# A reserve of early products, a decay multiplied on POOL and joint state updates in a hybrid mixer layer

## The chip, the cores and the metric

The kernel runs on one core of one Trainium2 chip. The metric is the device time of one execution in microseconds (us), lower is better. Five engines work side by side, each in the order of its own instructions: TensorE (PE, with its weight loads as PEld), VectorE (DVE), ScalarE (ACT), GpSimd (POOL) and SyncE (SP), which here issues nearly all transfers, one after the other.

## The reference

One layer of a diffusion backbone on 384 tokens (128 of context, 256 latent), width 2048, in fp32:

```python
h = rmsnorm(x, norm_g) * (1 + scale) + shift          # shift, scale, gate = silu(c) @ ada_w + ada_b
z = h @ w_in                                          # 2048 -> some 18,800 columns
# branch A, 32 heads of 64, two directions, per token t:
sa = S @ a_t
S  = S * w_t[None, :] + sa[:, None] * b_t + v_t[:, None] * k_t
y  = S @ r_t                                          # directions summed, group norm, + bonus
y_a = (norm(y) * silu(g_a)) @ w_out_a
# branch B: short convolution
y_b = (b_gate * conv3(c_gate * x_b) * silu(g_b)) @ w_out_b
out = x + gate * ((sigmoid(m_a) * y_a + sigmoid(m_b) * y_b) @ w_o)
```

The latent scans start from cached states; the final states of the context scans are outputs too. The outputs are the two token groups and the two final states.

## The kernel before

Every large product is made from three reduced-precision products (`mm3`, L81 to L83): a matrix is split into a high and a low part (`split`, L88 the high one on ACT, L89 the low one on DVE), and hi x hi, lo x hi and hi x lo are added in PSUM. A *triple* is these three matmuls for one block of 128 x 128 weights and 384 tokens.

**Prologue.** Eight groups g produce the modulated input `h_hi`/`h_lo`, two of its 16 blocks of 128 rows each. For each group four chunks of adaLN weights (`raw_adah`, 2 transfers of 512 KB, five buffers) are multiplied on PE (L289); `make_h` (L349 to L361) turns the rows by four small matmuls, and DVE and ACT modulate the block and split it. Between the chunks `pops(n)` places *early products*: triples of seven column tiles of w_in that need only the blocks which are there already (`pe`, 14 a group, from a queue). What is left of them stands behind the last `make_h`. Then begins a stream of weights.

**Stream.** `ds_.go(n)` places n triples of the big projection (pairs of column tiles of rk, gv, bc, bx, bg, gb, ma, mb, and ob of w_out_b at the end). `urgent` and `fills` hold what comes next; the weights of a pair are transferred one half at a time (`raw`, two buffers).

**Scan.** Sixteen iterations b, each with a pair of heads, use the stream as filler. In chunks of 64 tokens, six a direction: `prep_a` makes keys `bk`, decays `ep` and others, for the next b; `prep_b` makes pA = bk x pr (L687), masks it on DVE (L693) into A, sends triangles to DRAM, inverts them on DVE (L708, L710, 30 steps, tile U), copies the result on POOL (UT, L714) and loads x and A back; `prep_c` transposes bk into `bt` (pb, L754). `scan` begins with a *corner*: pH (L789), copies of x alternating ACT and DVE (L795), H0 = 5 triples, pbn and bon, pX (L789), copies of A (L806), H1 triples. Then two chains walk through the chunks of context (two) and latent tokens (four): po (L827), addition to sav (L828), ls = decayed state (L832, ACT), ytok (L837, L839), pq (L844), copy to sav (L846), pu (L851), new state st (L855 or L857). CH0 triples stand between the steps of the chains while both run, CH1 for the rest of the longer one. `norm` (L896 to L906) and `finish` (L912 to L917) follow, the latter inside the next iteration. An iteration has WINDOW = 80 triples ahead of its scan, FIRST more in the first, LAST in the last; 160 in all in most of them.

At the end the products with w_out_b (ob), w_out_a (oa), the gate rows and w_o follow; `load_yb` and `load_ya` (L500 to L502) bring branch results back from DRAM and split them.

PE's order is the order in which the program is written. That of the other engines is decided by a scheduler, which gives the scan precedence (`high_priority`).

Of the kernel before, what the change touches and what calls it, by code (L numbers as in the profile page):

```python
# [12 lines left out]
ALU = mybir.AluOpType  # L13
AX = mybir.AxisListType

P = 128
# [4 lines left out]
NB = 16  # L21
C = 64
NCH = 6
# [33 lines left out]
def hybrid_step(ctx, tc, cst, x_prompt, x_sample, state_f, state_b, c, c_ctx, ada_w, ada_b, norm_g,  # L57
# [32 lines left out]
        return hi, lo  # L90


    PB0, PB1, H0, H1, CH0, CH1 = 14, 6, 5, 4, 2, 3
    PRO, WINDOW, FIRST, LAST = 32, 80, 12, 16

    def wload(view, k0, cols, nm):

# [267 lines left out]
    def pops(n):  # L365
        for _ in range(n):
            if queue:
                early_mm(*queue.pop(0))

    for g in range(8):  # L370
        m5 = pp.tile([NSEL, 512], F32, tag="m5", name=f"m5_{g}", bufs=2)
        pa = pps.tile([P, 512], F32, tag="ada", name=f"pada_{g}")
        ac = [(256 * g, 256), (D + 256 * g, 256)]
        steps = ada_rows(condw, m5, ac, pa, lambda i: ada_load(pp, f"h{g}", ac, i, 5))
        for j in range(4):
            next(steps)
            if g == 0:
                if j < 3:
                    x_norm(j)
                    x_turn(j)  # L380
                else:
                    make_par()
            if j == 1:
                hl = early_load(g)
            pops(4 if j < 2 else 3)
        make_h(g, m5, pa)
        queue += [(2 * g + e, hl, i) for e in range(2) for i in range(NE)]


# [179 lines left out]
    st = []  # L569
# [87 lines left out]
    def prep_b(b, o):  # L657
# [23 lines left out]
        for d in range(2):  # L681
# [14 lines left out]
            for e in range(2):  # L696
                es = slice(32 * e, 32 * e + 32)
                for h in range(2):
                    hs = slice(C * h + 32 * e, C * h + 32 * e + 32)
                    nc.sync.dma_start(ui[d, e, h::2].rearrange("i s t -> s i t"), A[es, NCH * d:NCH * d + NCH, 0, hs])  # L700

        U = sp.tile([48, 32, 32], F32, tag="U", name=f"U_{b}")
        nc.sync.dma_start(U[:], ui[:].rearrange("d e i s t -> (d e i) s t"))
        ut = sp.tile([48, 256], F32, tag="ut", name=f"ut_{b}")
# [75 lines left out]
    def scan(b, o):  # L780
# [34 lines left out]
        def chain(ch):  # L815
            ls = None
            for i in range((2, 4)[ch]):
                n0 = [((0, 2), (4, 0))[d][ch] + i for d in range(2)]
                f0, step = n0[0], NCH + n0[1] - n0[0]
                fs, ff = slice(f0, f0 + step + 1, step), [f0, f0 + step]  # L820
                lam = [o["ep"][d][:, f % NCH, C:C + 1] for d, f in enumerate(ff)]
                zero = ch == 0 and i == 0
                need_state = ch == 0 or i < 3
                if not zero:
                    po = bank(f"po_{b}_{ch}_{i}")
                    for d, f in enumerate(ff):
                        TE.matmul(po[:, d, :], o["pr"][d][:, f % NCH, :], st[ch][:, d, :], start=True, stop=True)  # L827
                    V.tensor_tensor(sav[0:C, fs, :], po[0:C, 0:2, :], sav[0:C, fs, :], ALU.add)  # L828
                    if need_state:
                        ls = sp.tile([P, 2, P], F32, tag=f"lam{ch}", name=f"ls_{b}_{ch}_{i}")  # L830
                        for d in range(2):
                            S.mul(ls[:, d, :], st[ch][:, d, :], lam[d])  # L832
                    for d, f in enumerate(ff):
                        m = f if d == 0 else 5 - f % NCH
                        dst = ytok[hss[m % 2], m // 2, :]
                        if m in written:
                            V.tensor_tensor(dst, po[C:P, d, :], dst, ALU.add)  # L837
                        else:
                            S.copy(dst, po[C:P, d, :])  # L839
                        written.add(m)  # L840
                    yield 0
                pq = bank(f"pq_{b}_{ch}_{i}")
                for d, f in enumerate(ff):
                    TE.matmul(pq[:, d, :], A[:, f, 0, :], sav[:, f, :], start=True, stop=True)  # L844
                for h in range(2):
                    S.copy(sav[0:C, fs, hss[h]], pq[hss[h], 0:2, hss[h]])  # L846
                yield 0
                if need_state:
                    pu = bank(f"pu_{b}_{ch}_{i}")
                    for d, f in enumerate(ff):  # L850
                        TE.matmul(pu[:, d, :], bt[:, f, :], sav[:, f, :], start=True, stop=True)  # L851
                    for d in range(2):
                        for hs in hss:
                            if zero:
                                V.tensor_scalar(st[ch][hs, d, hs], pu[hs, d, hs], lam[d][hs], None, ALU.mult)  # L855
                            else:
                                V.scalar_tensor_tensor(st[ch][hs, d, hs], pu[hs, d, hs], lam[d][hs],  # L857
                                                       ls[hs, d, hs], ALU.mult, ALU.add)
                    yield 0

        live = [chain(1), chain(0)]
# [71 lines left out]
    for b in range(NB):  # L933
        if b < NB - 1:
            if b > 0:
                ds_.urgent += [(add_rk, b + 1), (add_gv, b)]
        else:
            ds_.urgent += [(add_gv, b)]
        if b == NB - 2:
            ds_.fills += [(add_ob, g) for g in range(8)]  # L940
        pb_gen = prep_b(b, cur)
        ds_.go(next(pb_gen))
        if prev is not None:
# [196 lines left out]
```

## Time and profile before

| | us |
|---|---|
| median of 3 runs | 2289.15 (2288.56 to 2292.72) |
| the profiled execution | 2289.19 |
| its span | 2287.4 |
| PE busy | 2215.7 (97%) |
| DVE busy | 1577.0 (69%) |
| ACT busy | 1017.4 (44%) |
| POOL busy | 104.8 (5%) |

The span is the time from the first to the last instruction; 1.8 us lie around it. The page's slices (a fortieth of the span, 57.2 us, each) show the DMA engines busy at nine tenths or more in the first two, at 335 and 346 GB/s, and at 109 to 134 GB/s in most of the middle. PE shows nine tenths or more in all slices but the first and the last. Busy time of PE counts a matmul from its start to a modelled end: a matmul that is held up halfway counts as busy.

### The profile page before, as it was taken

The page shows a single profiled execution, that of the slowest core. Times are in us where ns is not written, and L with a number is a line of the kernel's source. Part 1 is how long each engine was busy: PE and PEld are TensorE (multiplying, and loading weights), DVE is VectorE, ACT ScalarE, POOL GpSimd, SP SyncE. Part 2 cuts the span into 40 slices and gives each one's busy share as a digit, 9 for nine tenths or more (in the row PEclk, how much of TensorE's full clock was granted, in tenths as well). Part 3 has the DMA queues.
Part 4 walks back from the last instruction along what each step waited for, and adds up shares of the span by engine and source line. Part 5 has one row for each costly group of instructions (what it writes and reads, how often), then busy time and mean ns, then how long its engine had stood idle before and what let it go on. Part 6 is the DMA issues. An engine that isn't in the chain of part 4 may idle for free.

```text
span 2287.4 us, 40741 instructions
## 1 busy us (share of the span) xinstructions
PE 2215.7 (97%) x16084; PEld 2085.5 (91%) x16084; DVE 1577.0 (69%) x3256; ACT 1017.4 (44%) x1836; POOL 104.8 (5%) x99
## 2 busy tenths in 40 slices
PE   6999999999999999999999999999999999999998
PEld 4678899999999999999999999999999999989988
DVE  3248777887777878787878777777778675444444
ACT  4236344444545445444544454545444543333233
POOL 2000000000000000000000000000000000000000
PEclk9999999999999999999999999999999999999999
DMA  9963344434343434343444434444434466786633
GB/s 335 346 190 109 115 110 119 113 113 129 106 119 119 122 108 129 107 125 97 128 111 121 125 115 134 124 126 124 134 112 135 128 217 193 243 299 196 225 129 114
DMA packets 431695, 339.99 MB, mean 149 GB/s; under 512 B 86848, under 2 KB 413072, under 8 KB 430608
## 3 DMA queue, kind: packets, MB, share of 16 engines
q1 hardware_dynamic: 430016, 335.63, 49.1%
q8 instruction: 127, 2.08, 0.4%
q10 hardware_dynamic: 432, 1.57, 0.2%
q14 instruction: 64, 0.52, 0.1%
q0 software_dynamic: 1056, 0.19, 0.1%
HBM read 307.37 MB, written 29.36 MB: 147 GB/s over the span
## 4 chain that ended last, share of the span: by engine, by line
PE 75%; DVE 14%; DMA 4%; ACT 4%; issue 2%; SPq 1%; POOL 0%; POOLq 0%; DVEq 0%; ACTq 0%
PE d_rk L81 3%; PE d_rk L82 3%; PE d_rk L83 3%; PE d_gv L82 3%; PE d_gv L81 3%; PE d_gv L83 3%; DVE st L857 2%; PE d_oa L81 2%; PE pA L687 2%; PE d_oa L83 2%; PE d_oa L82 2%; PE d_bc L81 2%; PE d_ob L81 2%; PE d_ob L83 2%; PE d_ob L82 2%
## 5 line engine op out<-in xcount | busy, mean ns | idle before, releaser
L708 DVE TENSOR_TENSOR ut<-U 48x30 f32<-48x30 f32 (+14 forms) x480 | 154.1, 321 | 18.8 <-DMA U<-ui 7.4
L81 PE MATMUL d_rk<-h_hi,whi_rk 128*128 128x384 f32 x480 | 161.0, 335 | 0.6 <-ACT lst L547 0.6
L81 PE MATMUL d_gv<-h_hi,whi_gv 128*128 128x384 f32 x480 | 161.3, 336 | 0.0
L82 PE MATMUL d_gv<-h_lo,whi_gv 128*128 128x384 f32 x480 | 161.1, 336 | 0.0
L83 PE MATMUL d_gv<-h_hi,wlo_gv 128*128 128x384 f32 x480 | 161.1, 336 | 0.0
L710 DVE TENSOR_TENSOR U<-U,ut 48x30 f32<-48x30 f32 (+14 forms) x480 | 153.8, 320 | 10.1
L82 PE MATMUL d_rk<-h_lo,whi_rk 128*128 128x384 f32 x480 | 160.5, 334 | 0.0
L83 PE MATMUL d_rk<-h_hi,wlo_rk 128*128 128x384 f32 x480 | 160.4, 334 | 0.0
L88 ACT CAST whi_gv<-raw_gv 128x1024 fp32r<-128x1024 f32 (+1 forms) x64 | 64.0, 1000 | 137.0 <-PE d_rk L82 96.4
L89 DVE TENSOR_TENSOR wlo_rk<-raw_rk,whi_rk 128x1024 fp32r<-128x1024 f32 x60 | 73.2, 1223 | 73.9 <-ACT whi_rk L88 73.2
L88 ACT CAST whi_rk<-raw_rk 128x1024 fp32r<-128x1024 f32 x60 | 62.7, 1049 | 91.1 <-PE d_rk L82 28.1
L81 PE MATMUL d_bg<-h_hi,whi_bg 128*128 128x384 f32 x256 | 93.4, 365 | 2.4 <-DVE bc L460 2.4
L81 PE MATMUL d_bc<-h_hi,whi_bc 128*128 128x384 f32 x256 | 93.3, 365 | 0.0
L81 PE MATMUL d_ma<-h_hi,whi_ma 128*128 128x384 f32 x256 | 93.3, 364 | 0.0
L89 DVE TENSOR_TENSOR wlo_oa<-raw_oa,whi_oa 128x1024 fp32r<-128x1024 f32 x32 | 39.2, 1224 | 78.4 <-ACT whi_oa L88 78.4
L81 PE MATMUL d_mb<-h_hi,whi_mb 128*128 128x384 f32 x256 | 93.0, 363 | 0.0
L81 PE MATMUL d_gb<-h_hi,whi_gb 128*128 128x384 f32 x256 | 92.8, 363 | 0.0
L81 PE MATMUL d_bx<-h_hi,whi_bx 128*128 128x384 f32 x256 | 92.1, 360 | 0.0
L81 PEld LDWEIGHTS d_rk<-h_hi,whi_rk 128*128 128x128 f32 x480 | 90.1, 188 | 1.0 <-ACT lst L547 0.9
L81 PEld LDWEIGHTS d_gv<-h_hi,whi_gv 128*128 128x128 f32 x480 | 90.8, 189 | 0.0
L82 PEld LDWEIGHTS d_gv<-h_lo,whi_gv 128*128 128x128 f32 x480 | 90.8, 189 | 0.0
L83 PEld LDWEIGHTS d_gv<-h_hi,wlo_gv 128*128 128x128 f32 x480 | 90.7, 189 | 0.0
(319 smaller groups left out, 6676.6 us busy)
## 6 DMA issues: line engine op xcount, KB each, us to landing
raw_adah<-in_ada_w_dram SPq DMA_DIRECT2D x64, 512.0 KB, 8.7
raw_rk<-in_w_in_dram SPq DMA_DIRECT2D x60, 512.0 KB, 5.4
raw_gv<-in_w_in_dram SPq DMA_DIRECT2D x60, 512.0 KB, 4.5
raw_bc<-in_w_in_dram SPq DMA_DIRECT2D x16, 1024.0 KB, 5.4
raw_bx<-in_w_in_dram SPq DMA_DIRECT2D x16, 1024.0 KB, 5.4
raw_bg<-in_w_in_dram SPq DMA_DIRECT2D x16, 1024.0 KB, 5.4
raw_gb<-in_w_in_dram SPq DMA_DIRECT2D x16, 1024.0 KB, 5.5
raw_ma<-in_w_in_dram SPq DMA_DIRECT2D x16, 1024.0 KB, 5.5
```

What stands on the lines that cost most here:

```text
L81: TE.matmul(out, wh, xh, start=start, stop=False)
L82: TE.matmul(out, wh, xl, start=False, stop=False)
L83: TE.matmul(out, wl, xh, start=False, stop=stop)
L88: S.copy(hi[0:rows], src)
L89: V.tensor_tensor(lo[0:rows], src, hi[0:rows].bitcast(F32), ALU.subtract)
L687: TE.matmul(pas[h, n // 4 * 4][:, n % 4, :], bk[hss[h], n, :], pr[hss[h], n, :], start=True, stop=True)
L708: V.tensor_tensor(tv, U[:, 0:s, s:s + 1].broadcast_to([48, s, w]), U[:, s:s + 1, s + 1:].broadcast_to([48, s, w]), ALU.mult)
L710: V.tensor_tensor(U[:, 0:s, s + 1:], U[:, 0:s, s + 1:], tv, ALU.add)
L857: V.scalar_tensor_tensor(st[ch][hs, d, hs], pu[hs, d, hs], lam[d][hs], ls[hs, d, hs], ALU.mult, ALU.add)
```

## The change

1. *Prologue.* `pops` places 3, 4, 3 and 2 early products behind the four chunks and 2 behind `make_h` (before: 4, 4, 3, 3 and none); in group 1 two behind each. Six products more stay in the queue from there on, and stand behind the last `make_h`.
2. *Decay.* The state update multiplied pu and the old state by the chunk's decay `lam`. Now POOL multiplies the keys `bk` by it once per direction and iteration (128 x 768), behind pA and ahead of the transposes; pu then holds the decay already.
3. *State update.* Four DVE operations on 64 x 64 become two on 64 x 2 x 64: a copy in the first step of the context chain, else an addition of ls.
4. *Numbers.* H1 4 to 2, CH1 3 to 4, FIRST 12 to 24.
5. *Queue.* The last `add_gv` is placed ahead of the eight `add_ob` at b = 14, not as urgent at b = 15.

```diff
@@ -90,8 +90,8 @@
         return hi, lo
 
 
-    PB0, PB1, H0, H1, CH0, CH1 = 14, 6, 5, 4, 2, 3
-    PRO, WINDOW, FIRST, LAST = 32, 80, 12, 16
+    PB0, PB1, H0, H1, CH0, CH1 = 14, 6, 5, 2, 2, 4
+    PRO, WINDOW, FIRST, LAST = 32, 80, 24, 16
 
     def wload(view, k0, cols, nm):
 
@@ -382,8 +382,10 @@
                     make_par()
             if j == 1:
                 hl = early_load(g)
-            pops(4 if j < 2 else 3)
+
+            pops(2 if g == 1 else (3, 4, 3, 2)[j])
         make_h(g, m5, pa)
+        pops(2)
         queue += [(2 * g + e, hl, i) for e in range(2) for i in range(NE)]
 
 
@@ -699,6 +701,9 @@
                     hs = slice(C * h + 32 * e, C * h + 32 * e + 32)
                     nc.sync.dma_start(ui[d, e, h::2].rearrange("i s t -> s i t"), A[es, NCH * d:NCH * d + NCH, 0, hs])
 
+        for d in range(2):
+            G.tensor_tensor(o["bk"][d][:], o["bk"][d][:], o["ep"][d][:, :, C:C + 1].broadcast_to([P, NCH, P]), ALU.mult)
+
         U = sp.tile([48, 32, 32], F32, tag="U", name=f"U_{b}")
         nc.sync.dma_start(U[:], ui[:].rearrange("d e i s t -> (d e i) s t"))
         ut = sp.tile([48, 256], F32, tag="ut", name=f"ut_{b}")
@@ -849,13 +854,11 @@
                     pu = bank(f"pu_{b}_{ch}_{i}")
                     for d, f in enumerate(ff):
                         TE.matmul(pu[:, d, :], bt[:, f, :], sav[:, f, :], start=True, stop=True)
-                    for d in range(2):
-                        for hs in hss:
-                            if zero:
-                                V.tensor_scalar(st[ch][hs, d, hs], pu[hs, d, hs], lam[d][hs], None, ALU.mult)
-                            else:
-                                V.scalar_tensor_tensor(st[ch][hs, d, hs], pu[hs, d, hs], lam[d][hs],
-                                                       ls[hs, d, hs], ALU.mult, ALU.add)
+                    for hs in hss:
+                        if zero:
+                            V.tensor_copy(st[ch][hs, :, hs], pu[hs, 0:2, hs])
+                        else:
+                            V.tensor_tensor(st[ch][hs, :, hs], pu[hs, 0:2, hs], ls[hs, :, hs], ALU.add)
                     yield 0
 
         live = [chain(1), chain(0)]
@@ -934,10 +937,8 @@
         if b < NB - 1:
             if b > 0:
                 ds_.urgent += [(add_rk, b + 1), (add_gv, b)]
-        else:
-            ds_.urgent += [(add_gv, b)]
         if b == NB - 2:
-            ds_.fills += [(add_ob, g) for g in range(8)]
+            ds_.fills += [(add_gv, NB - 1)] + [(add_ob, g) for g in range(8)]
         pb_gen = prep_b(b, cur)
         ds_.go(next(pb_gen))
         if prev is not None:
```

On DVE, the corner of iteration 12 before (kd and kn belong to the next iteration's keys, `x` to L795, `A` to L806):

```order
L649 TENSOR_SCALAR kd_0_16080<-sig_2_16047,par,omka 128x384
L636 RECIPROCAL kn_16070<-kn_16070 128x128
L795 COPY x_12_15583<-pH_16092 32x6x32
L636 RECIPROCAL kn_16070<-kn_16070 128x128
L795 COPY x_12_15583<-pH_16092 32x6x32
L636 RECIPROCAL kn_16070<-kn_16070 128x128
L802 TENSOR_TENSOR bon_16149<-pbn_16146,v_14809 128x384
L637 SCALAR_TENSOR_TENSOR kn_16070<-kk_15975,kn_16070 128x384
L806 COPY A_15419<-pX_16151 32x6x32
L650 TENSOR_TENSOR kd_0_16080<-k_15837,kd_0_16080 128x384
L806 COPY A_15419<-pX_16151 32x6x32
L651 TENSOR_TENSOR sig_2_16047<-kn_16070,sig_2_16047 128x384
```

and after:

```order
L651 TENSOR_SCALAR kd_0_16110<-sig_2_16077,par,omka 128x384
L638 RECIPROCAL kn_16100<-kn_16100 128x128 x3
L800 COPY x_12_15625<-pH_16122 32x6x32
L639 SCALAR_TENSOR_TENSOR kn_16100<-kk_16005,kn_16100 128x384
L800 COPY x_12_15625<-pH_16122 32x6x32
L652 TENSOR_TENSOR kd_0_16110<-k_15867,kd_0_16110 128x384
L653 TENSOR_TENSOR sig_2_16077<-kn_16100,sig_2_16077 128x384
L807 TENSOR_TENSOR bon_16179<-pbn_16176,v_14847 128x384
L646 SCALAR_TENSOR_TENSOR L_1_16114<-cs,sig_1_16053 128x384
L811 COPY A_15459<-pX_16181 32x6x32
L89 TENSOR_TENSOR wlo_mb_0_0_16166<-raw_mb_0_16163,whi_mb_0_0_16165 128x1024
L833 TENSOR_TENSOR sav_15640<-po_1_0_16217,sav_15640 64x2x128
L811 COPY A_15459<-pX_16181 32x6x32
```

The three reciprocals stand together ahead of the first copy of x, one multiplication stands between the two copies of x, and four operations between the second of them and the first copy of A.

On DVE, the early state updates of iteration 12 before (`st_1144` and `st_1146` are the states of the two chains, `sig`, `kd` and `bk` parts of the next keys):

```order
L89 TENSOR_TENSOR wlo_ma_0_1_16140<-raw_ma_0_16133,whi_ma_0_1_16139 128x1024
L651 TENSOR_TENSOR sig_3_16059<-kn_16070,sig_3_16059 128x384
L855 TENSOR_SCALAR st_1144<-pu_0_0_16230,ep_1152 64x64 x2
L855 TENSOR_SCALAR st_1144<-pu_0_0_16230,ep_1154 64x64 x2
L666 TENSOR_TENSOR bk_0_16498<-kd_0_16080,sig_0_16011 128x6x64
L857 SCALAR_TENSOR_TENSOR st_1146<-pu_1_0_16246,ep_1152,ls_1_0_16197 64x64 x2
L857 SCALAR_TENSOR_TENSOR st_1146<-pu_1_0_16246,ep_1154,ls_1_0_16197 64x64 x2
```

and after:

```order
L667 TENSOR_TENSOR bk_1_16539<-sig_3_16089,sig_1_16053 128x6x64
L668 TENSOR_TENSOR bk_1_16539<-kd_1_16118,sig_1_16053 128x6x64
L775 TENSOR_TENSOR kd_0_16110<-kd_0_16110,kd_1_16118 128x384
L859 COPY st_1144<-pu_0_0_16254 64x2x64 x2
L89 TENSOR_TENSOR wlo_mb_0_1_16170<-raw_mb_0_16163,whi_mb_0_1_16169 128x1024
L861 TENSOR_TENSOR st_1146<-pu_1_0_16265,ls_1_0_16221 64x2x64 x2
```

The second update moves behind a split, and the keys' operations ahead of the first.

On PE, the last `make_h` of the prologue before (`pada` is its PSUM tile, `pe` the banks of the early products, `ehi` and `elo` their weights, numbered by group):

```order
L81 MATMUL pe_101<-h_hi_79,ehi_6_830 128x384
L82 MATMUL pe_101<-h_lo_83,ehi_6_830 128x384
L83 MATMUL pe_101<-h_hi_79,elo_6_831 128x384
L349 MATMUL pada_896<-cs,m_7_895 128x2
L350 MATMUL pada_896<-cs,m_7_895 128x2
L349 MATMUL pada_896<-cs,m_7_895 128x2
L350 MATMUL pada_896<-cs,m_7_895 128x2
L81 MATMUL pe_95<-h_hi_79,ehi_7_930 128x384
L82 MATMUL pe_95<-h_lo_83,ehi_7_930 128x384
L83 MATMUL pe_95<-h_hi_79,elo_7_931 128x384
L81 MATMUL pe_96<-h_hi_79,ehi_7_930 128x384
```

and after:

```order
L81 MATMUL pe_95<-h_hi_79,ehi_6_815 128x384
L82 MATMUL pe_95<-h_lo_83,ehi_6_815 128x384
L83 MATMUL pe_95<-h_hi_79,elo_6_816 128x384
L349 MATMUL pada_884<-cs,m_7_883 128x2
L350 MATMUL pada_884<-cs,m_7_883 128x2
L349 MATMUL pada_884<-cs,m_7_883 128x2
L350 MATMUL pada_884<-cs,m_7_883 128x2
L81 MATMUL pe_96<-h_hi_79,ehi_6_815 128x384
L82 MATMUL pe_96<-h_lo_83,ehi_6_815 128x384
L83 MATMUL pe_96<-h_hi_79,elo_6_816 128x384
L81 MATMUL pe_97<-h_hi_79,ehi_6_815 128x384
```

The products behind `make_h` are still of the group before (`ehi_6`), where they were of the new one (`ehi_7`).

## Rows read from the trace of the kernel before

**Rows 1.** Waits of PE: waited for what: us in total, times, longest us.
```profile
PE po L827 <- DVE st L857: 8.9, 14, 1.1
PE pe L81 <- ACT h_hi L360: 7.4, 8, 2.1
...
PE pH L789 <- DMA x<-uo: 5.2, 4, 2.2
PE py L912 <- DVE ytok L906: 3.0, 3, 1.6
...
PE d_ob L81 <- ACT whi_ob L88: 2.3, 1, 2.3
PE d_ob L83 <- DVE wlo_ob L89: 2.1, 2, 1.5
```

**Rows 2.** Groups, 400 to 1800: count, busy us, mean ns, idle before, releaser.
```profile
L857 DVE SCALAR_TENSOR_TENSOR st<-pu,ep,ls 64x64 f32<-64x64 f32 x210 | 59.4, 283 | 14.5 <-PE pu L851 9.5
...
L827 PE MATMUL po<-st,pr 128*128 128x128 f32 x264 | 54.7, 302 | 11.0 <-DVE st L857 8.4
...
L844 PE MATMUL pq<-sav,A 128*128 128x128 f32 x316 | 48.1, 274 | 0.8 <-DVE sav L828 0.8
...
L837 DVE TENSOR_TENSOR ytok<-po,ytok 64x128 f32<-64x128 f32 x54 | 15.9, 294 | 1.2
```

**Rows 3.** Timeline of PE, iteration 12: start, us, instruction, [idle before <- releaser].
```profile
1575.05 1.02 PE L827 MATMUL po<-st,pr 128*128 128x128 f32 x4 [0.46 <-DVE st L857]
```

**Rows 4.** Prologue end: SP issues, transfers from 100 to 140, timeline of PE.
```profile
121.03 4.74 SPq L275 DMA_DIRECT2D raw_adah<-in_ada_w_dram  x4
...
raw_adah<-in_ada_w_dram SPq DMA_DIRECT2D x14, 512.0 KB, 8.5
...
136.74 1.07 PE L289 MATMUL pada<-raw_adah,condw_pro 128*32 128x512 f32 x8
...
150.82 0.33 PE L81 MATMUL pe<-h_hi,ehi 128*128 128x384 f32 x1
...
151.34 0.33 PE L81 MATMUL pe<-h_hi,ehi 128*128 128x384 f32 x1
...
152.64 0.45 PE L81 MATMUL d_rk<-h_hi,whi_rk 128*128 128x384 f32 x1 [0.61 <-ACT lst L547]
```

**Rows 5.** Stretches: us, busy us (x instructions) of five engines, PEclk, DMA share, GB/s.
```profile
369.00:373.00 4.00, 4.00 (x16) 3.97 (x14) 3.88 (x8) 1.36 (x2) 0.00 (x0) 0.57 0.75 254
262.00:266.00 4.00, 1.85 (x55) 1.50 (x54) 1.57 (x2) 0.52 (x3) 0.00 (x0) 1.00 0.79 202
```

**Rows 6.** Corner of iteration 12, timelines of DVE, then PE.
```profile
1551.50 0.94 DVE L636 RECIPROCAL kn<-kn 128x128 f32<-128x128 f32 x1
...
1553.84 0.36 DVE L795 COPY x<-pH 32x192 f32<-32x192 f32 x1
...
1554.25 0.62 PE L789 MATMUL pX<-A,x 32*32 32x32 f32 x48
...
1558.49 0.61 PE L844 MATMUL pq<-sav,A 128*128 128x128 f32 x4
```

**Rows 7.** Corner of iteration 1, timeline of DVE.
```profile
367.28 2.57 DVE L636 RECIPROCAL kn<-kn 128x128 f32<-128x128 f32 x3
...
370.85 0.36 DVE L795 COPY x<-pH 32x192 f32<-32x192 f32 x1
```

**Rows 8.** Timelines: POOL and DVE after an inversion; PE around pA and pb.
```profile
1641.04 2.07 POOL L714 COPY UT<-U 48x1024 f32<-48x1024 f32 x1 [26.84 <-DVE U L710]
...
1641.06 3.15 DVE L89 TENSOR_TENSOR wlo_ma<-raw_ma,whi_ma 128x1024 fp32r<-128x1024 f32 x1
1645.21 1.22 DVE L89 TENSOR_TENSOR wlo_ma<-raw_ma,whi_ma 128x1024 fp32r<-128x1024 f32 x1 [1.01 <-ACT whi_ma L88]
...
1494.59 1.61 PE L687 MATMUL pA<-pr,bk 64*128 64x128 f32 x24
...
1501.07 0.60 PE L754 MATMUL pb<-cs,bk 128*128 128x128 f32 x4
```

## The prediction

> **What bounds the kernel now.** I read the page's shares first: TensorE (PE) is busy 97% of a 2287.4 us span, VectorE (DVE) 69%, so only what PE waits for, or runs slowly through, can be won. Then the waits of PE [rows 1]: none is over 12 us in total, and six of them are near this change (8.9 for the state, 5.2 for x, 3.0 for ytok, 7.4 for h_hi, 2.3 and 2.1 for w_out_b). A matmul that stops between its parts shows no wait, only a longer time, so the groups of the middle come next [rows 2]: po and pq are the same matmul shape, 302 ns against 274. At the pq rate 264 po would take 264 x 48.1/316 = 40.2 us; they take 54.7, so 14.5 us hide inside po, and 11.0 of idle stand ahead of them: 25.5 us in 13.1 iterations, 1.9 each. A late step of iteration 12 shows it [rows 3]: po stands 0.46 us for the DVE's st, and then takes 1.02 us for its four matmuls, where pq takes 0.61 [rows 6], because the second direction's st ends still later.
>
> The profiled run took 2289.19 us, 0.04 from the median of the runs, so the sum is made from 2289.2.
>
> **State update.** Five updates an iteration go from four operations on 64 x 64 (283 ns each, 1.1 us together) to two on 64 x 128. The ytok addition has that shape and those operands, 294 ns [rows 2], so 0.6 us, about half. The decay that they no longer apply goes to POOL. po of the late steps missed its place by at most 0.46 + (1.02 - 0.61) = 0.87 us [rows 3]; 0.5 is saved there and the long direction's fill grows from three triples to four (one triple of matmuls is 0.52 us, from 150.82 to 151.34 in [rows 4]), together 1.0. In the early steps the excess is 0.2 to 0.3, under 0.5. DVE is occupied without a pause from the corner to there, and in the new order the second early update stands behind a 1.22 us split [rows 8]; adding up its operations puts its end at 1566.2 where po wants it at 1566.1, so 0.1 stays in some iterations. I take 24 of the 25.5; the bounds are 12 (only half of each wait goes) and 25.5. The triples in an iteration stay 160, so moving them costs no matmul.
>
> **Decay on POOL.** Two products of 128 x 768 an iteration. No row shows one. Bounds: the DVE's own rate for a two-operand 128 x 1024 (1.22 us [rows 8]) gives 0.92; POOL's copy of 48 x 1024 in 2.07 us gives 1.55; the worst is one that takes 3.1 like the disturbed split of the same rows. I take 1.55. The keys are last read by the second pA, which begins at 1494.59 and ends near 1496.2, and are next read by the transposes from 1501.07 [rows 8]: 4.9 us, and the first product can begin with the first half, 4.8 us sooner. Even 3.1 for the second is covered. If the DVE's masks of pA were held as well, U and with it x would come up to 3 us later; x is waited for in four iterations only [rows 1], so two or three would feel it. Cost taken: 0, bounds 0 to 5.
> What the two engines do to each other is seen where POOL's UT copy and a DVE split start together [rows 8]: 2.07 us on POOL, and 3.15 on the DVE instead of 1.22, so the one ran after the other. The Trainium skill, "GPSIMD Engine Reference", section 1 (Specifications) and section 8 (Key points), says that the two share their SBUF interfaces, and that DVE instructions with two SBUF inputs contend; this trace agrees. The masks read one operand from PSUM: by that rule they would not be held and the sum stays; were they held, it would be 5 us more. [...]
>
> **The corner.** This is what the change costs. Now nothing waits there: in iteration 12 pX starts at 1554.25, just after the DVE's second copy of x has ended (1553.84 + 0.36) [rows 6]. Before, the three reciprocals (0.94 each) alternate with the x copies. In the new order, in iterations 3, 5, 7 and 9 to 14, all three stand first, then copy, multiply, copy. Iteration 1 of before already has this order: three reciprocals from 367.28, last copy ended at 370.85 + 0.36 = 371.21, 3.93 us later [rows 7]. From 1551.50 that is 1555.43, and pX, whose fourth small matmul needs that copy, stops for 1555.43 + 0.05 - 1554.25 = 1.23 us (in iteration 1 it cost nothing only because pX came at half clock). The fill after pX falls by two triples, but pq still comes at 1558.49 + 1.23 - 1.05 = 1558.67 [rows 6], and the A copy that it needs ends at 1558.2 (1555.46, then kd, sig, bon at 0.47 each, a scan of 0.97, the copy 0.36): no second stop. In iterations 4 and 8 a split of 1.22 stands ahead of that A copy: 1.05 more, 2.3. In 2 and 6 one more product of 0.5 stands between the x copies and pq waits 0.55: 2.35. Iteration 0: 1.2. Sum 9 x 1.23 + 2 x 2.3 + 2 x 2.35 + 1.2 = 21.6 us. Bounds: 11 (if the last copy slips ahead of the multiply) and 34 (every iteration at 2.3).
>
> **First iterations.** FIRST = 24 gives iterations 0 and 1 12 and 16 triples (6 and 8 us) more ahead of pH: the waits of 2.2 and 1.4 go, 3.5 in all. The other 1.7 of pH's 5.2 [rows 1] only changes iterations, since H1 = 2 takes 2.1 us ahead of pH from the rest. The stop of 1.4 also lowered the clock: 369 to 373 has 0.57 granted, that is level 1.2 for most of it, (1 - 0.57) x 4.00 = 1.7 us [rows 5]. Gain 5.2.
>
> **Prologue.** The last four adaLN chunks are issued from 121.03 to 125.8, the last near 124.6, and take 8.5 to land: 133.1. PE uses it at 136.74, so PE is 3.6 behind there, not the transfers [rows 4]. With six products in reserve PE arrives at 136.74 - 6 x 0.525 = 133.6. After it come 1.0 (chunk), two products, make_h 1.0 and twenty products at 0.525: 147.1, with h_hi covered by the reserve (six products, 3.15, against a wait of 2.1). Before, the fourteen products that follow begin only after that wait, and the stream begins at 152.64, 0.61 after them [rows 4]. That last wait, for copies out of the banks, stays, so the stream begins at 147.7: gain 5.0, bounds 0 (rival 3) and 5.5. The waits for h_hi of the earlier groups bring nothing, as the transfers pace those groups.
>
> **ob and the end.** add_gv moves ahead of ob: the split wait of 1.5 us at ob's start (of the 2.1 in [rows 1]) goes, its 16 subtractions now stand among the masks of iteration 15 and delay U by about 2. At the other end SP holds w_out_b back behind the loads of ya: PE waits 2.3 and 0.6 and the clock falls (1.7). One more half is issued ahead of those loads, and 54 triples (28 us) now lie between. Gain 4.6, bounds 0 and 4.6. In iterations 4 and 8 the normalisation's DVE work is queued later and py L912 waits 2.4 each, more than the 3.0 of three iterations now [rows 1] by about 2: cost 2.
>
> **Clock.** Stops of this size have met both ends: 1.4 at iteration 1 lowered it [rows 5], 2.2 at iteration 0 did not (1.00 from 262 to 266). Thirteen new stops at 1.7 each are 0 to 22; the two rows give an even chance, but in the second the stop was longer, so I take four: 6.8.
>
> **Sum.** Gains 24 + 5.2 + 5.0 + 1.5 + 4.6 = 40.3; costs 21.6 + 2 + 2 + 6.8 = 32.4. 2289.2 - 7.9 = 2281.3, forecast 2281.
>
> **Rivals.**
> 1. *The corner is not paid.* If the x copies still land in time, 21.6 and the dips go: 2281 - 28 = 2253; 2267 if half of it does. For it: the reciprocals wait for pn alone, and if that came some 1.2 us sooner they would be through. Against: pn and pH come in one stretch of PE's own order, which the change leaves as it is. 0.15.
> 2. *The clock falls at every stop* (slower). At 17 stops (13 of pX, four of pq) of 1.7 each that is 29 instead of 6.8: 2281 + 22 = 2303. From nine dips on nothing is left of the gain (4 + 7.9/1.7), from twelve on it is a loss that can be measured. For it: iteration 1, whose stop was as short. Against it: iteration 0. 0.18.
> 3. *The change does not do what it says*: po still waits, because what ends last there is the place of st in the DVE's queue, not the length of its operations. Then 12 of the 24 stay, 2293; and 2298 if the prologue keeps its time too. For it: the split that stands ahead of the second update. Against: [rows 3], where st itself is the last thing. 0.17.
> 4. *POOL holds the DVE's masks*: 2286. 0.05.
>
> **How the numbers follow.** The forecast has what is left, 0.45, and its own range is 2274 to 2287. 0.2% (4.6 us) is about what a measurement of this kernel can tell from no change. Faster, under 2284.6: 0.40 of the forecast's 0.45 and rival 1, 0.55. Same, to 2293.8: the 0.05 left of the forecast, rival 4, and 0.13 of rival 3, 0.23. Slower: rival 2 and the rest of rival 3, 0.22. The range reaches from a little below the half case of rival 1 to nearly the whole of rival 2: 2262 to 2301; it leaves out some 0.05 below and 0.1 above.
>
> **What would show it.** The po group near 275 ns with its idle under 2 us between 400 and 1800 (state update); a wait of pX on x copies of 1.2 us in nine iterations, and reciprocals in threes (corner); the stream beginning near 147.7 (prologue); no wait for x in iterations 0 and 1; POOL products under 3 us and ended before the transposes; no wait for whi_ob near the end; the number of stretches of PE at half clock in the middle (four or so). I am wrong if pX does not wait, or if po keeps its idle time.

## The result, and the profile after

The changed kernel takes 2272.43 us (median of four runs, 2270.96 to 2274.91); the kernel before, run beside it, 2288.86 (2287.80 to 2292.72). The ratio is 0.9926, with an interval of 0.9909 to 0.9943: faster by 0.7%, 16.4 us. The forecast was 2281, a gain of 7.9, so the sign was right and the size half. The time lies below the 2274 to 2287 that the prediction gave for its own mechanism, and inside the wider 2262 to 2301. The profiled execution took 2274.91, the longest of the four and 14.3 less than that of before; the account below is made between these two.

The page's first part (busy us of each engine, its share of the span of 2273.1 us), and the waits of PE of the changed kernel (waited for what: us in total, times, longest us):

```profile
PE 2201.9 (97%) x16084; PEld 2079.6 (91%) x16084; DVE 1539.6 (68%) x3096; ACT 1012.6 (45%) x1836; POOL 156.4 (7%) x131
```
```profile
PE pH L794 <- DMA x<-uo: 7.5, 7, 1.6
...
PE pX L794 <- DVE x L800: 4.5, 10, 1.1
...
PE pq L849 <- DVE A L811: 1.8, 3, 0.7
...
PE d_ob L81 <- ACT ybh L503: 1.3, 1, 1.3
PE d_ob L81 <- DVE smb L516: 1.0, 1, 1.0
PE pe L81 <- ACT h_hi L360: 1.0, 1, 1.0
PE po L832 <- DVE st L861: 0.8, 5, 0.2
PE d_ob L82 <- DVE ybl L504: 0.7, 2, 0.5
PE d_ob L81 <- ACT whi_ob L88: 0.7, 1, 0.7
PE d_ob L83 <- DVE wlo_ob L89: 0.6, 1, 0.6
...
PE py L915 <- DVE ytok L909: 0.5, 2, 0.2
```

PE is still what bounds it, at the same share. Beside [rows 1], the wait for the state has gone from 8.9 to 0.8 us, those for h_hi and ytok are nearly gone; a wait of pX on the copies of x is new (4.5, ten times), and the wait of pH for x has grown from 5.2 in four iterations to 7.5 in seven. Groups of the middle, 400 to 1800, to be read against [rows 2] (instructions | busy us, mean ns | idle before):

```profile
L849 PE MATMUL pq<-sav,A 128*128 128x128 f32 x318 | 48.5, 274 | 1.8 <-DVE A L811 1.8
...
L832 PE MATMUL po<-st,pr 128*128 128x128 f32 x268 | 42.1, 279 | 1.2 <-DVE st L861 0.8
L705 POOL TENSOR_TENSOR bk<-bk,ep 128x768 f32<-128x768 f32 x26 | 39.0, 1501 | 100.8 <-PE pA L689 97.4 <-DMA ui<-A 3.3
```

po now runs at pq's rate. Its excess is 42.1 - 268 x 48.5/318 = 1.2, with the idle 2.4 in all, against 25.5 before.

The corner of iteration 12, DVE and then PE, against [rows 6] (start, us, instruction, [idle before <- releaser]):

```profile
1553.16 2.57 DVE L638 RECIPROCAL kn<-kn 128x128 f32<-128x128 f32 x3
1555.76 0.35 DVE L800 COPY x<-pH 32x192 f32<-32x192 f32 x1
1556.14 0.56 DVE L639 SCALAR_TENSOR_TENSOR kn<-kk,kn 128x384 f32<-128x384 f32 x1
1556.73 0.36 DVE L800 COPY x<-pH 32x192 f32<-32x192 f32 x1
```
```profile
1555.91 0.83 PE L794 MATMUL pX<-A,x 32*32 32x32 f32 x6
1557.14 0.57 PE L794 MATMUL pX<-A,x 32*32 32x32 f32 x42 [0.39 <-DVE x L800]
```

pX begins, stands until the copy that ends at 1557.09, and only then does its other 42 products. It begins at 1555.91; all of it would have been over 0.62 later [rows 6], at 1556.53, and ends at 1557.71: a stop of about 1.2.

x itself comes later. Transfers, 400 to 1800, of before and then after (count, size, median us from issue to landing):

```profile
U<-ui SPq DMA_DIRECT2D x13, 192.0 KB, 2.8
uo<-U SPq DMA_DIRECT2D x13, 192.0 KB, 3.3
...
A<-uo SPq DMA_DIRECT2D x104, 24.0 KB, 1.9
x<-uo SPq DMA_DIRECT2D x26, 48.0 KB, 1.9
```
```profile
U<-ui SPq DMA_DIRECT2D x13, 192.0 KB, 4.9
...
A<-uo SPq DMA_DIRECT2D x104, 24.0 KB, 4.7
x<-uo SPq DMA_DIRECT2D x26, 48.0 KB, 3.9
```

The load of U takes 2.1 us longer, the loads of A and x 2.8 and 2.0. What is near them on SP's queue in iteration 12, before and then after:

```profile
1501.36 0.31 SPq L703 DMA_DIRECT2D U<-ui  x1
1503.70 1.02 SPq L104 DMA_DIRECT2D raw_gv<-in_w_in_dram  x2
```
```profile
1504.42 0.39 SPq L104 DMA_DIRECT2D raw_gv<-in_w_in_dram  x1
1505.05 0.39 SPq L708 DMA_DIRECT2D U<-ui  x1
```

Before, the two halves of the gv weights were issued behind the load of U; now one of them is issued 0.6 us ahead of it. The same is seen ahead of the loads of A and x, in iterations 1 to 14. The kernel before has a half there, 0.5 us ahead, in iterations 1, 5 and 9 alone: x lands 53.0, 55.4 and 55.7 us after the end of pA in these, 47.9 to 51.1 in the others from 2 to 14, and these are three of the four iterations in which its pH waits.

### The profile page after: what moved, and what is told of

Same layout as the page of the kernel before. It is cut to its first block, busy times and chain, and to the rows that moved or that the text cites. A ratio compares the mean times of both kernels' runs of the same rounds, so it can differ in the third digit from the quotient of the medians.

```text
span 2273.1 us, 40714 instructions
## 1 busy us (share of the span) xinstructions
PE 2201.9 (97%) x16084; PEld 2079.6 (91%) x16084; DVE 1539.6 (68%) x3096; ACT 1012.6 (45%) x1836; POOL 156.4 (7%) x131
## 3 DMA queue, kind: packets, MB, share of 16 engines
q10 hardware_dynamic: 432, 1.57, 0.2%
## 4 chain that ended last, share of the span: by engine, by line
PE 79%; DVE 11%; DMA 6%; issue 2%; ACT 1%; SPq 1%; POOL 0%; POOLq 0%; DVEq 0%; ACTq 0%
DMA raw_adah<-in_ada_w_dram 4%; PE d_rk L81 3%; PE d_rk L83 3%; PE d_rk L82 3%; PE d_gv L81 3%; PE d_gv L82 3%; PE d_gv L83 3%; PE d_oa L81 2%; PE pA L689 2%; PE d_oa L83 2%; PE d_oa L82 2%; PE d_gb L81 2%; PE d_gb L83 2%; PE d_gb L82 2%; PE d_mb L81 2%
## 5 line engine op out<-in xcount | busy, mean ns | idle before, releaser
L715 DVE TENSOR_TENSOR U<-U,ut 48x30 f32<-48x30 f32 (+14 forms) x480 | 153.9, 321 | 10.3
L81 PE MATMUL d_ob<-ybh,whi_ob 128*128 128x384 f32 x256 | 89.1, 348 | 3.0 <-ACT ybh L503 1.3
```

The source lines that it names most:

```text
L81: TE.matmul(out, wh, xh, start=start, stop=False)
L715: V.tensor_tensor(U[:, 0:s, s + 1:], U[:, 0:s, s + 1:], tv, ALU.add)
```

## The experiments

My theory (A in the expectations) after this: the gain is the state update's; the rest of the change is eaten where its numbers move pH and pX, by the corner and by x that comes later, since SP issues a weight's half ahead of it. The rivals (B, C): the delay of x is POOL's doing; the numbers pay and the corner costs nothing; or one small part carries the gain. The numbers were not tried alone in the kernel before, nor was the order on SP moved by itself.

Times of before in the same jobs were 2289.93 (e1 to e4), 2292.19 (e5 to e8) and 2291.80 (e9 to e12); each ratio is to these. The parts are numbered as in the change.

**e1: parts 2 and 3 alone**, in the kernel before.

```
+        for d in range(2):
+            G.tensor_tensor(o["bk"][d][:], o["bk"][d][:], o["ep"][d][:, :, C:C + 1].broadcast_to([P, NCH, P]), ALU.mult)
...
+                        if zero:
+                            V.tensor_copy(st[ch][hs, :, hs], pu[hs, 0:2, hs])
+                        else:
+                            V.tensor_tensor(st[ch][hs, :, hs], pu[hs, 0:2, hs], ls[hs, :, hs], ALU.add)
```

> The kernel before with the decay on POOL and the joint state update alone (parts 2 and 3), all numbers as before. Theory A (the shorter state update is worth most of the gain by itself): the time inside and ahead of po falls from 25.5 us to 6 to 10 us, some is left in the late steps since their fill stays three triples; about 2270 us. Rival B (po waits for the place of st on the DVE, or needs the longer fill): under 8 us gained, 2281 or more. Rival C (POOL's products hold U back): U lands 2 us later after pA as in the changed kernel, and pH waits for x in more than four iterations; A and B expect U to land 7.9 us after the end of pA as before.

Measured: 2273.00, ratio 0.9918 (0.9903 to 0.9933). This is the whole gain of the changed kernel. Its po group, 400 to 1800:

```profile
L830 PE MATMUL po<-st,pr 128*128 128x128 f32 x260 | 41.8, 283 | 6.5 <-DVE st L859 6.5
```

The stop inside po is gone with the joint update alone: 41.8 - 260 x 48.6/316 = 1.8 of excess. What is left is idle ahead of it, 6.5, which the fourth triple of CH1 takes away in the full change. The load of U takes 2.9, as before, and pX waits 0.6 in all: the corner and the late x do not come with the decay.

**e2: part 1 alone.**

```
-            pops(4 if j < 2 else 3)
+            pops(2 if g == 1 else (3, 4, 3, 2)[j])
         make_h(g, m5, pa)
+        pops(2)
```

> The kernel before with the new distribution of early products alone (part 1). Theory A: the stream begins at 147.7 instead of 152.6 and the half clock stretches of the prologue but the first are gone; 2284 us (5 less). Rival: the transfers pace the prologue and the stream begins no sooner; 2289 us.

Measured: 2287.38, 0.9977 (0.9966 to 0.9989), 2.5 us of the 5. The first line is the start of the stream, 5.0 us sooner than 152.64 [rows 4]; the second a stretch of iteration 0 (us, busy us of five engines, PEclk, DMA share, GB/s):

```profile
147.64 0.45 PE L81 MATMUL d_rk<-h_hi,whi_rk 128*128 128x384 f32 x1 [0.61 <-ACT lst L549]
```
```profile
257.00:264.00 7.00, 6.13 (x50) 5.80 (x53) 0.71 (x2) 0.62 (x2) 0.00 (x0) 0.52 0.36 125
```

The prologue does give 5.0. PE then comes to pH of iteration 0 sooner and waits longer for x (in all 7.0 against 5.2), and 257 to 264 runs at the lower level, 1.2 GHz, for nearly all of the 7 us: half of the gain is gone in the median, and more between the profiled executions, which are 1.2 apart.

**e3: the changed kernel with the old H1 and CH1** (FIRST stays 24).

```
-    PB0, PB1, H0, H1, CH0, CH1 = 14, 6, 5, 2, 2, 4
+    PB0, PB1, H0, H1, CH0, CH1 = 14, 6, 5, 4, 2, 3
```

> The changed kernel with H1 = 4 and CH1 = 3 as before, FIRST stays 24. Theory A (H1 and CH1 moved the phase of the weight stream against the scan: one half of weights came to stand ahead of U and of the loads of x on SP's queue, and the reciprocals ahead of the copies of x): no stop of pX in iterations 4 and 6 to 14, pH waits for x in at most three iterations, U lands 7.9 us after pA again; 9 us of pH and 11 of pX are saved and some 6 to 8 us come back at po: 2260 to 2264. Rival B (the longer fill of the long chain is worth more than it costs): 2272 or more. Rival C (POOL holds U): U lands at 9.9 as in the changed kernel.

Measured: 2272.99, 0.9924 (0.9909 to 0.9939): the same as the changed kernel, 9 or more off what was expected. The mechanism in the middle was as expected: from iteration 4 on pH and pX stop in iterations 5 and 9 only, 0.8 us each, and U lands 8.0 to 8.3 us after the end of pA as before (9.8 to 10.3 in the changed kernel). But po waits again (5.7, twelve times), and its first iterations wait up to 1.9 for x at pH (7.3 in all, six times) with a lowered clock behind two of them. What the corner costs is about what CH1 = 4 brings.

**e4: H0 = 7, H1 = 0**, to give the corner time by moving pX back by two triples.

```
-    PB0, PB1, H0, H1, CH0, CH1 = 14, 6, 5, 2, 2, 4
+    PB0, PB1, H0, H1, CH0, CH1 = 14, 6, 7, 0, 2, 4
```

> The changed kernel with H0 = 7 and H1 = 0: the two triples behind pX stand ahead of it, nothing else moves. Theory A (pX stops only because the last copy of x ends 1.2 us too late): the stop falls from 1.2 to 0.2 us in some nine iterations, 2262 us. Rival B (the stop only moves to pq, which waits for the copy of A): pq waits about 1 us in those iterations and the time stays 2270 to 2273.

Measured: 2285.92, 0.9981 (0.9970 to 0.9993), 0.55% or 12.6 us above the changed kernel's ratio. The wait of PE that grew most (that of pH for x grew too, to 10.6), and the corner on DVE in iteration 12:

```profile
PE pq L849 <- DVE A L811: 17.8, 12, 2.2
```
```profile
1565.01 1.20 DVE L89 TENSOR_TENSOR wlo_mb<-raw_mb,whi_mb 128x1024 fp32r<-128x1024 f32 x1
...
1566.72 0.41 DVE L833 TENSOR_TENSOR sav<-po,sav 64x256 f32<-64x256 f32 x1
1567.15 0.35 DVE L811 COPY A<-pX 32x192 f32<-32x192 f32 x1
```

The number does not only move PE: the DVE's order follows, a split of 1.20 and the sum into sav slip ahead of the copy of A, and pq, which needs it, stands for up to 2.2.

**e5 and e6: H1 = 4 with CH1 = 4**, that is four triples at the corner without taking them from po; e6 also has the old FIRST.

```
-    PB0, PB1, H0, H1, CH0, CH1 = 14, 6, 5, 2, 2, 4
-    PRO, WINDOW, FIRST, LAST = 32, 80, 24, 16
+    PB0, PB1, H0, H1, CH0, CH1 = 14, 6, 5, 4, 2, 4
+    PRO, WINDOW, FIRST, LAST = 32, 80, 24 (e5) or 12 (e6), 16
```

> The changed kernel with H1 = 4, CH1 = 4, FIRST = 24. It differs from the next kernel in FIRST alone, that is in the phase of the weight stream against the scan: here one half of weights stands ahead of U and another ahead of x on SP's queue in iterations 2 to 14. Theory A (that place on the queue is what makes x late): pH waits 1 to 2.5 us for x in most of iterations 2 to 14, 15 us or more in all, and the time is 2272 to 2280 us. Rival B (the place on the queue does not matter, x is late for its own reasons or not at all): waits like those of the next kernel, and a time within 3 us of it.

> The changed kernel with H1 = 4, CH1 = 4 and FIRST = 12: no half of weights stands ahead of U or of x in iterations 0 to 14. Theory A: no wait for x from iteration 2 on, no stop of pX (the reciprocals are over before pH), nothing left at po; 2256 to 2262 us. Rival B (stops come back at the corner for other reasons, as at pq with H0 = 7): 2268 or more.

Measured: e5 2293.72, 1.0004 (0.9993 to 1.0016); e6 2294.55, 1.0019 (1.0004 to 1.0034). Both lose the whole gain. The waits expected of e5 came, its time did not, and what I expected of e6, a version that beats both, fell. The wait of pH for x in e5, then in e6:

```profile
PE pH L794 <- DMA x<-uo: 23.2, 18, 3.4
```
```profile
PE pH L794 <- DMA x<-uo: 12.4, 11, 3.0
```

In e6 pX adds 8.9 of its own, and the layer's products `pl` 10.7 for their split weights. In e6 no half of a weight is issued ahead of the loads of U or of x, which land after 2.9 and 2.0 us, yet the stores of U into `uo` take 4.3 instead of 3.3, and x is late all the same. So the place on SP makes half of the waits for x (23.2 against 12.4) and is not their only cause. In the trace of e6 each step between pA and x is late: counted from the end of pA, in the median of iterations 2 to 14, the stores of A into `ui` land at 6.3 us (before 5.1), those of U into `uo` at 44.7 (42.0) and x at 53.0 (48.5), while pH comes at 52.1 (54.3). Why they are late was not separated. The profiled execution of e6 took 2289.65, 4.9 less than its median, so its waits are not all that the others had.

**e7: part 5 alone.**

```
-        else:
-            ds_.urgent += [(add_gv, b)]
...
-            ds_.fills += [(add_ob, g) for g in range(8)]
+            ds_.fills += [(add_gv, NB - 1)] + [(add_ob, g) for g in range(8)]
```

> The kernel before with part 5 alone (the last gv pair ahead of ob). Theory A (the forecast's terms: 1.5 at the start of ob and 4.6 at the second load of branch results go, 2 come back in iteration 15): 2285 to 2286 us. Rival B (the waits for w_out_b only change their place, as the changed kernel still has 4.3 us of them): 2288 to 2291.

Measured: 2291.28, 0.9998 (0.9987 to 1.0009). No gain: the waits for whi_ob and wlo_ob are still 2.0 and 2.1, and pH waits 7.7 instead of 5.2.

**e8: all copies of x on ACT**, so that pX does not depend on the DVE.

```
-            (S.copy, V.tensor_copy)[j % 2](x11[32:64, j::4, :], pz[j])
+            S.copy(x11[32:64, j::4, :], pz[j])
```

> The changed kernel with all four copies of x on ScalarE. Theory A (pX stops because two copies of x wait behind the DVE's reciprocals): pX no longer stops, 10 to 11 us less, 2262 us. Rival B (the DVE's backlog moves the stop on, as with H0 = 7: pq waits for the copy of A): pq waits 10 us or more and the time is 2270 to 2278.

Measured: 2271.42, 0.9913 (0.9892 to 0.9935), no different from the changed kernel. The waits after it:

```profile
PE pH L794 <- DMA x<-uo: 10.4, 8, 1.8
PE pq L849 <- DVE A L811: 5.2, 8, 0.8
```

pX stops nowhere now, which is worth 11.1 us, but 3.4 of it come back one step later, at the copy of A (1.8 to 5.2), and 2.9 at pH (7.5 to 10.4). The rest shows in the profiled execution, 4.4 shorter than that of the changed kernel, and hardly in the medians, 1.0 apart. So a part of the corner's cost is the DVE's backlog, which the next copy has to wait out; that all of it is, is not shown.

**e9: parts 1, 2 and 3**, without the numbers and the queue (e1 and e2 together).

> The kernel before with parts 1, 2 and 3 (early products, decay on POOL, joint state update); H1, CH1, FIRST and the gv pair stay as before. Theory A (parts add, and parts 4 and 5 of the change bring nothing on balance): the prologue's 2.5 to 5 us come off the 2273 of the state update alone, 2268 to 2271, that is no slower than the whole change. Rival B (parts 4 and 5 are needed for the whole gain): 2276 or more.

Measured: 2271.08, 0.9912 (0.9897 to 0.9926); this is the changed kernel's ratio within the intervals. Parts 4 and 5 bring nothing on balance.

**e10 and e11: e9 with one triple moved** in the late steps of the long chain, from behind pq to behind pu; e11 also has FIRST = 16.

```
+                    shift[0] = 0      # after po
...
+                shift[0] = -1         # after pq
...
+                    shift[0] = 1      # after pu
...
-                    yield CH0 if len(live) > 1 else CH1
+                    yield CH0 if len(live) > 1 else CH1 + shift[0]
```

> As the kernel with parts 1, 2 and 3, but in the steps of the longer chain that run alone one triple is moved from behind pq to behind pu, ahead of the next po, so that po has four triples ahead of it and the sum of triples is unchanged. Theory A (what was left at po with CH1 = 3, 0.9 us an iteration, is the late steps, and they can have their triple without shifting the weight stream): po has nothing left, iterations of 104.6 us, no waits for x after iteration 1; 2256 to 2262 us. Rival B (the triple is missed behind pq, where sav is awaited, or the DVE's order turns at the corner): 2268 or more.

> The same with FIRST = 16 instead of 12: four triples more ahead of the first pH. Theory A: the waits for x in iterations 0 and 1 (about 2 us each) and the half clock behind them shrink; 2 to 4 us less than with FIRST = 12. Rival B (x of the first iterations only moves along): within 1.5 us of it.

Measured: e10 2260.74, 0.9864 (0.9850 to 0.9879); e11 2259.71, 0.9860 (0.9845 to 0.9874). Both beat before, by 31 to 32 us, and the changed kernel: 2272.43 - 2260.74 = 11.7 by the times, and the intervals of the ratios are apart. e11 is within 1.5 us of e10, as its rival said. But the gain is not by what I wrote: po still waits, 7.2 us, fourteen times (in e9 7.1, fourteen times). The late step of iteration 12 that waits, DVE and PE of e10, then PE of e9:

```profile
1549.12 1.23 DVE L89 TENSOR_TENSOR wlo_ma<-raw_ma,whi_ma 128x1024 fp32r<-128x1024 f32 x1 [0.90 <-PE pu L858]
1550.38 0.61 DVE L863 TENSOR_TENSOR st<-pu,ls 64x128 f32<-64x128 f32 x2
```
```profile
1551.13 0.68 PE L832 MATMUL po<-st,pr 128*128 128x128 f32 x4 [0.47 <-DVE st L863]
```
```profile
1558.82 0.68 PE L832 MATMUL po<-st,pr 128*128 128x128 f32 x4 [0.44 <-DVE st L861]
```

The moved triple does not reach this step. It is the one at which the short chain has just ended, and in both kernels po has three triples ahead of it, CH0 = 2 and CH1 - CH0 = 1; the po that did get a fourth is the next one, and it waits in neither. A split of 1.23 stands ahead of the update in e9 as in e10, so st ends late in both. My expectation that po has four triples ahead of it was wrong of the one po that waits; the changed kernel, with CH1 = 4, has four there. The gain over e9 lies elsewhere: the waits for ytok (2.5) and at pX (0.6) are gone, pH's falls from 5.5 to 4.4, those at d_ob from 4.7 to 3.9, in all 5.0; and the mean granted clock of the span rises from 0.994 to 0.996, 4.5 us of 2260 (give or take 2.3, as it is rounded to 0.001). Together that is about the 9.6 us between the two profiled executions. The edit also left one triple fewer behind pH than I had counted, since the last pq of a chain has no pu behind it; pH so comes half a microsecond later (54.85 us after the end of pA, in e9 54.33), which fits the smaller waits and was not tried by itself.

**e12: the decay's products on the DVE** instead of POOL, in the changed kernel.

```
-            G.tensor_tensor(o["bk"][d][:], ...
+            V.tensor_tensor(o["bk"][d][:], ...
```

> The changed kernel with the two products of keys and decay on VectorE instead of POOL. Theory A (the products are hidden on POOL, and the DVE has room for 2 us there, between the masks and U): 2270 to 2275 us. Rival B (on POOL they hold the DVE or SP up, so U lands late because of them): U lands at 7.9 us after pA instead of 9.9, and the time falls by 5 us or more. Rival C (the DVE is too full): U or the transposes come later, 2278 or more.

Measured: 2282.06, 0.9959 (0.9944 to 0.9973), slower than the changed kernel. Its transfers, and the wait that is new:

```profile
U<-ui SPq DMA_DIRECT2D x13, 192.0 KB, 4.7
...
x<-uo SPq DMA_DIRECT2D x26, 48.0 KB, 4.0
```
```profile
PE pb L759 <- DVE bk L705: 4.1, 1, 4.1
```

With POOL out of it U and x land as late as in the changed kernel, so POOL is not what delays them. The place on POOL is worth 0.9959 - 0.9926, some 7.6 us, from runs that were not made side by side. One product takes the DVE 0.95 (946 ns); the transposes of the last iteration wait 4.1 for it, and pH waits 2.7 longer in all (8.6 for x and 1.6 for `sig`).

## Why the prediction was half right

**Right: state update.** 24 taken, 25.5 - 2.4 = 23.1 measured. e1 shows that the joint update alone gives about 17 and CH1 the rest. The forecast read the step that po missed by most from iteration 12; in iterations 2, 4, 6 and 8 po stood 1.1 (the longest of [rows 1]), and this went too. Rival 3 did not come in the changed kernel; the wait that e1, e9 and e10 have left is just what it described, a split of 1.23 ahead of st in iteration 12.

**Right: prologue.** The stream begins here:

```profile
147.76 0.45 PE L81 MATMUL d_rk<-h_hi,whi_rk 128*128 128x384 f32 x1 [0.61 <-ACT lst L549]
```

147.7 was forecast, 4.9 of 5.0 came, and by the path that was forecast. PE comes to the last chunk at 133.0 (133.6 forecast), waits 0.46 for its transfer (133.1 forecast) and has so caught up with the transfers:

```profile
133.46 1.06 PE L289 MATMUL pada<-raw_adah,condw_pro 128*32 128x512 f32 x8 [0.46 <-DMA raw_adah<-in_ada_w_dram]
```

e2 shows what the sum left out: what arrives sooner waits longer for x, unless FIRST moves pH too.

**Right: POOL.** POOL and DVE in iteration 12:

```profile
1495.24 1.52 POOL L705 TENSOR_TENSOR bk<-bk,ep 128x768 f32<-128x768 f32 x1 [5.04 <-PE pA L689]
```
```profile
1495.33 1.94 DVE L695 TENSOR_TENSOR A<-pA,cs 128x512 f32<-128x512 f32 x4
```

1.52 us (1.55 taken) beside four masks that take 1.94 together, two of 512 elements at 0.68 and two of 256 at 0.41 (the line gives the form of the first): the two run through each other's time, and neither took turns as the copy and the split of [rows 8] did. The masks read one operand from PSUM; the Trainium skill, "GPSIMD Engine Reference", section 8 (Key points), names DVE instructions in a 2-port perf mode or with two SBUF inputs as those that contend, and the trace agrees. Rival 4 is out as it was put. But in iteration 0, beside two splits, which have two SBUF inputs, the product takes 3.64, more than the 3 us that the forecast had named as a sign. And in iteration 1 the DVE's operation on two SBUF tiles ahead of the masks takes 1.57 beside the product, where it takes 0.34 by itself; the masks come late, and from the start of the first pA to the end of the second are 8.1 us instead of 6.5 before (6.9 in e12, without POOL). That is some 1.2 us where the forecast took 0.

**Half right: the corner, 21.6 forecast, 12.9 measured.** The mechanism and the price were right where it came: the reciprocals stand in threes, and the stop (the time of pX less 0.62) is 1.02 to 1.18 in iterations 5, 7 and 9 to 14, 1.32 in iteration 0 and 0.48 in 6, together 11.1. The second stop at pq came in 4, 6 and 8, 1.8 in all, where 3.2 was forecast for 2, 4, 6 and 8. The stop of pX was forecast for 2, 3, 4 and 8 too and did not come there: the step that failed is that pH was taken to run as before. In those four iterations PE itself was held at pH by a late x, as here in iteration 3 (the second half of pH):

```profile
592.26 0.39 PE L794 MATMUL pH<-x,A 32*32 32x32 f32 x24 [1.65 <-DMA x<-uo]
```

and by the time pX came the reciprocals were over. Two delays of about one size stood in parallel and were added up. Rival 1 rested on the reciprocals' being over in time, and gave that 0.15; it was so in these four iterations, because pH came late and not because pn came early.

**Wrong: pH, 3.5 gain forecast, 2.3 loss measured.** The waits of iterations 0 and 1 went with FIRST = 24, as said, and those of 5 and 9 went too, but 2, 3, 4, 6 and 8 wait now. The step that failed is that the other 1.7 of pH's waits "only changes iterations": it moved pH 2.1 us earlier and left x where it was. In iteration 12 x lands 3.8 us later, measured from the end of pA (52.1 instead of 48.3), and pH comes 2.1 earlier (52.25 instead of 54.33): a reserve of 6 us became 0.2. The longer part of this was in neither the diff nor the sum: the new numbers change which weights' halves are issued ahead of U and x on SP. Comparing SP's order of both kernels around those loads would have shown it beforehand. e12 rules POOL out as its cause; e1 and e9, which keep the numbers, have U at 2.9 and 2.8; e6 shows that the place on SP is not all of it.

**Wrong: py, 2 loss forecast, 2.5 gain measured.** ytok is waited for 0.5 now. I counted the waits of two iterations that the order makes later, and not that every new stop of PE at pH and pX gives the DVE time to catch up; that this is the reason was not tried by itself.

**Wrong: ob and the end, a net gain of 4.1 forecast (1.5 + 4.6 - 2), some 1.6 loss measured.** The waits at d_ob changed names, not size: 1.3 + 1.0 + 0.7 + 0.7 + 0.6 = 4.3, against 2.3 and 2.1 of [rows 1]. ob now starts directly behind work that ends late, so it waits for its operand ybh and the splits where it waited for weights. The clock's fall moved with it and costs more: 1818 to 1826 has 0.57 granted, (1 - 0.57) x 8 = 3.4 us, against (1 - 0.57) x 4 = 1.7 from 1946 to 1950 before. The step that failed named the wait that goes and not the one that is next behind it; part 5 by itself, in e7, brought no gain either.

**Near: clock.** Four new dips were taken, 6.8. Windows of the changed kernel (columns as in [rows 5]):

```profile
369.00:373.00 4.00, 4.00 (x25) 4.00 (x24) 2.24 (x5) 3.29 (x7) 0.00 (x0) 1.00 0.38 53
...
1818.00:1824.00 6.00, 5.25 (x27) 3.85 (x28) 5.76 (x12) 4.76 (x11) 0.00 (x0) 0.58 0.83 240
484.00:488.00 4.00, 3.48 (x34) 3.41 (x35) 3.88 (x8) 0.73 (x3) 0.00 (x0) 0.57 0.90 270
1554.00:1558.00 4.00, 3.50 (x62) 2.88 (x61) 3.87 (x8) 2.19 (x6) 0.00 (x0) 1.00 0.52 169
```

The dip at 369 is gone, as said. No stop of pX lowered the clock (1.00 from 1554 to 1558, with the stop in it); two waits for x did (484 and 593), and the start of ob. So rival 2 is out, but four (of thirteen; the forecast's own list of iterations has fourteen stops of pX) was too many for the corner and none had been put at the new waits of pH. Over the whole span the granted clock rose, from 0.991 to 0.994: four stretches at the lower level between 65 and 148 are gone with the waits for h_hi (0.57 from 144 to 148 in the last; they count in the prologue's gain). A longer one from 178 to 186 (0.57) has become a shorter one from 173 to 177 (0.59), which the sum did not have.

**The sum as it came**: po -23.1, the dip at 369 -1.7, prologue -4.9, py -2.5; corner +12.9, pH +2.3, two dips behind waits for x +3.4, ob and the end +1.6. That is -12.0 of the -14.3 between the profiled executions. What is left is not taken apart; po outside of 400 to 1800, the shorter dip at 173 (-1.8) and the second pA of iteration 1 (+1.6) are in it. The forecast's error of 6.4 there has the corner (8.7 too dear), py (4.5 too dear) and the dips (6.8 taken, 3.4 came) on one side, pH and ob and the end (5.8 and 5.7 too good) on the other. Five terms that missed by 3 to 9 us each largely cancel, so that the sign and half of the size came out is in part luck; the state update and the prologue came as forecast.

## What to carry to other kernels

Where a number moves a stop on one engine, ask first whether that engine will be held just ahead of it by something else: stops in a row on one path are not added, the later ones are absorbed. Where a change alters fill counts, compare the order of every queue, the one that issues transfers first of all, since a large weight load that slips ahead of a small load on which the path waits costs microseconds that no diff shows. And take the parts apart by runs: here two of five gave all of the gain, and moving one triple gave some 10 us more through terms that nobody had in the sum, not at the wait for which it was moved. To see whether such a move reaches its wait, count the filler ahead of that one instruction in the trace.

## What the hardware showed that was not expected

The product with a broadcast operand on POOL takes 1.50 us for 128 x 768 in the mean, beside the DVE's masks (1.52 and 1.49 in iteration 12), which are not longer for it, while the DVE itself needs 0.95 for it in e12. Beside DVE instructions with two SBUF inputs one runs behind the other: the product takes 3.64 where two splits began with it, and in e10 a multiplication into `ya` of 128 x 384 that began after the product takes 1.31 in most iterations, 0.56 by itself. The lowered clock did not follow the length of a stop alone: stops of 1.2 at pX left it at 1.00, a wait of 1.65 at pH lowered it, waits of 1.5 and 1.4 at pH in iterations 4 and 8 did not, and before, one of 2.2 did not and one of 1.4 did [rows 5]. The landing of a 24 KB load went from 1.9 to 4.7 us where the order of the transfers around it changed, with the same transfers in all.
